# Seventh product of every second Strassen unit: weights 64 bytes further on in their tile

## The chip, the cores and the metric

The kernel runs on one core of one Trainium2 chip. The metric is the device time of one execution in microseconds. Three runs of the kernel before gave 2523.32, 2526.15 and 2526.63 us; the median is 2526.15 us. The profiled execution is a run of its own.

## The reference

Two layers of a macaron block over one sequence of 512 tokens with 1024 channels. Each layer is a half-weighted feed-forward block, a mixer of three branches (RWKV-7 time mixing, chunked gated linear attention, cross-attention into 256 memory rows) merged under sigmoid gates, and a second feed-forward block:

```python
for l in range(DEPTH):                                   # DEPTH = 2
    x = x + 0.5 * swiglu_ffn(rmsnorm(x, ffn1_norm[l]), ffn1_w_in[l], ffn1_w_out[l])
    h = rmsnorm(x, mix_norm[l])
    ...                                                  # three branches, gates
    x = x + merged @ w_out[l]
    x = x + 0.5 * swiglu_ffn(rmsnorm(x, ffn2_norm[l]), ffn2_w_in[l], ffn2_w_out[l])
return rmsnorm(x, final_norm)

def swiglu_ffn(h, w_in, w_out):                          # D_FF = 2816
    gate, up = jnp.split(h @ w_in, 2, axis=-1)
    return (jax.nn.silu(gate) * up) @ w_out
```

What matters here are the three large products of a layer: `h @ w_in` and `... @ w_out` of the four feed-forward blocks, and `merged @ w_out` at the mixer's end. All is float32.

## The kernel before

All activations lie transposed: channels on the 128 partitions, the 512 tokens along the free axis. A float32 product is made from three products of the rounded type `float32r`: an operand is split into `hi`, its rounded value, and `lo`, the rest (`Net.split`: ScalarE writes `hi`, VectorE writes `lo`), and hi·hi, hi·lo and lo·hi are summed in PSUM.

The large products run as Strassen units (in the form with seven products). `Net.seven` (line 906) describes one unit. It takes weights as four blocks of n·128 columns per partition (n is 4, or 3 in the last third of the feed-forward's second product) and makes seven products of 256 tokens each. Their sums grow in three PSUM tiles, X, Y and Z. The unit is cut in three functions: `begin` makes the first two products, `middle` the next three, and `end` the last two. `Net.chain` (line 957) calls them so that `begin` of the next unit stands ahead of `end` of the present one. There are 30 units in each of the four feed-forward blocks (the first four columns of its first product are made without Strassen) and 4 at the end of each mixer, 128 in all.

`self.par7` turns with each unit, and `par` is its value for the unit; it is true for the first, third, fifth unit and so on. Before the change `par` chooses one thing alone, the PSUM tile of Z.

One product is `Net.part`: for each of the n weight blocks of 128x128 two matmuls with the rounded weights (against the operand's `hi` and `lo`), and then for each block one with the weights' rest, so 12 matmuls with n = 4, and 9 with n = 3. Each has a load of its weights of its own. The weights are the stationary operand, the activations (256 columns) stream.

`Net.piece` (line 839) makes the `hi` and `lo` of a block of weights. A pair of blocks gets two tiles from a shared pool. A single block (the fifth, sixth and seventh product of a unit) gets one tile `hl` with 64 + 2·512 numbers per partition from a ring of two (`fhl`); `hi` stands at `SHIFT` = 48 numbers, 192 bytes, from its start, and `lo` 512 numbers behind `hi`. The seventh product's weights come raw by a DMA on SyncE's queue into a tile `d` and need no sum of blocks, so `hl<-d` in the profile is the split of the seventh product's weights and nothing else. Its matmuls are those of ps_i (the tile of Y) with `hl`, just ahead of the next unit's `middle`.

The order of all instructions comes from a list scheduler in the kernel. `Recorder` notes every operation with its dependences (from which parts of a tile it reads and writes, `overlap`), `Recorder.cost` gives each a duration from engine, operation and element count, and `Recorder.plan` simulates the queues six times and keeps the shortest order. Matmuls are taken in the order in which they were noted, where they are ready. Because all operations are issued by one loop, the profile shows one line, L317, for nearly all of them, and groups are told apart by tiles.

Two small tiles exist for place alone: `shift` (48 numbers) and `level` (16 numbers), allocated in `setup` ahead of other pools. Places along a partition are the sum of the sizes that stand before.

Of the kernel before, what the change touches and what calls it, by code (L numbers as in the profile page):

```python
# [20 lines left out]
T = 512  # L21
# [10 lines left out]
SHIFT = 48  # L32
# [562 lines left out]
class Net:  # L595
# [240 lines left out]
        ops["t3"] = [(t3[0][:, q], t3[1][:, q]) for q in range(4)]  # L836
        return ops

    def piece(self, pool, raw):

        if raw.shape[1] == 2:
            hi, lo = (self.wp.tile(list(raw.shape), F32R, name=t[1:], tag=t, bufs=2) for t in ("whi", "wlo"))
        else:
            n = raw.shape[2]
            f = pool.tile([P, 64 + 2 * T], F32R, name="hl", tag="fhl", bufs=2)
            hi, lo = (f[:, SHIFT + i * T:SHIFT + i * T + n].rearrange("p (c t) -> p c t", c=1) for i in range(2))
        self.split(hi, lo, raw)
        return [(hi[:, c, :], lo[:, c, :]) for c in range(raw.shape[1])]

# [56 lines left out]
    def seven(self, pool, src, n, ops, evict, clear=False):  # L906


        nc, C = self.nc, n * P
        self.par7 = not self.par7  # L910
        par = self.par7
        ring = lambda tag, bufs, k=2: pool.tile([P, k, C], F32, name=tag, tag=tag, bufs=bufs)

        def begin():
            w = src.rearrange("p (c t) -> p c t", c=4)
            a = self.wp.tile([P, 2, C], F32, name="wraw", tag="wraw", bufs=3)
            nc.sync.dma_start(out=a, in_=w[:, 0:2])
            nc.gpsimd.dma_start(out=a[:, 1], in_=w[:, 3], accum_op=ALU.add)
            q = ring("q", NQ)
            nc.sync.dma_start(out=q[:, 1], in_=w[:, 2])  # L920
            e = ring("q", NQ)
            nc.sync.dma_start(out=e[:, 0], in_=w[:, 1])
            nc.gpsimd.dma_start(out=e[:, 0], in_=w[:, 0], accum_op=ALU.add)
            d = ring("d", 2, 1)
            nc.sync.dma_start(out=d, in_=w[:, 3:4])
            X, Y = self.big()[:, :H], self.small("i")[:, :H]
            Z = self.small("fc"[par])[:, :H]
            v = self.piece(pool, a)
            self.part(X, v[0], ops["b11"], True)
            if clear:  # L930
                nc.tensor.matmul(Y, v[0][0][:, :P], ops["b11"][0][0], start=True, stop=True)
            nc.scalar.activation(Y, X, AF.Copy)
            nc.vector.tensor_tensor(q[:, 0], a[:, 1], a[:, 0], ALU.add)
            self.part(Z, v[1], ops["n1"], True)
            evict("z1", Z)
            return q, e, d, X, Y, Z

        def middle(q, e, d, X, Y, Z):
            v = self.piece(pool, q)
            self.part(Y, v[0], ops["n2"], False)  # L940
            evict("u2", Y)
            nc.vector.tensor_tensor(e[:, 1], q[:, 0], q[:, 1], ALU.add)
            self.part(X, v[1], ops["b21"], False)
            evict("x", X)
            self.part(Y, self.piece(pool, e[:, 0:1])[0], ops["t3"], False)
            evict("u3", Y)
            return d, e, Y, Z

        def end(d, e, Y, Z):
            self.part(Z, self.piece(pool, e[:, 1:2])[0], ops["b22"], False)  # L950
            evict("z", Z)
            self.part(Y, self.piece(pool, d)[0], ops["t4"], False)
            evict("y", Y)

        return begin, middle, end

    def chain(self, jobs):
# [959 lines left out]
```

## Time and profile before

| what | us |
|---|---|
| median of three runs | 2526.15 |
| profiled execution, all | 2527.82 |
| its span, first to last instruction | 2526.0 |
| TensorE matmul busy | 2502.3 |
| TensorE weight load busy | 2265.2 |
| VectorE busy | 2100.2 |
| ScalarE busy | 1471.5 |
| GpSimd busy | 241.4 |

A busy time is the union of the instructions' spans on an engine. Matmuls overlap in the array, so the length of one says little of the pace; the pace is read from start to start, or from the chain of work, where a stretch of matmuls of one tile is given with its start, its length and its number. The time line lists single instructions in the same form.

### The profile page before, as it was taken

To read this page: it belongs to the slowest core of one execution; us is meant where nothing else is said; L and a number is where in the kernel's file an instruction comes from. 1 tells how busy PE (TensorE), PEld (TensorE's weight loads), DVE (VectorE), ACT (ScalarE), POOL (GpSimd) and SP (SyncE) were. 2 spreads that over 40 slices of the span, in tenths; PEclk is the share of its full clock that TensorE was granted. 3 is DMA by queue.
4 is the path that set the end of the run, shared out by engine and by line. 5 is a ranking of instruction groups with operands and counts; after the bars stand their busy time and mean duration, and the time that the engine had idled before them with its cause. 6 is when DMAs were issued, how large, how long until landed. Compare 5 with 4: busy or idle time off the path is not lost.

```text
span 2526.0 us, 47194 instructions
## 1 busy us (share of the span) xinstructions
PE 2502.3 (99%) x17636; PEld 2265.2 (90%) x17636; DVE 2100.2 (83%) x4218; ACT 1471.5 (58%) x2660; POOL 241.4 (10%) x364
## 2 busy tenths in 40 slices
PE   9999999999999999999999999999999999999998
PEld 8999988888888799999989999877887888899998
DVE  8988886678888689888899888766888877898888
ACT  6665666564544456565665656674745434565655
POOL 1111100000000001211111111000000000012110
PEclk9999999999999999999999999999999999999999
DMA  7787762322222556877657777523222225468774
GB/s 199 201 197 187 166 189 82 117 73 70 78 77 73 144 157 154 206 189 182 149 144 197 189 184 173 175 88 97 83 69 88 67 78 172 134 164 207 188 180 103
DMA packets 163668, 358.02 MB, mean 142 GB/s; under 512 B 18256, under 2 KB 38160, under 8 KB 163440
## 3 DMA queue, kind: packets, MB, share of 16 engines
q1 hardware_dynamic: 125344, 288.87, 36.7%
q0 software_dynamic: 36864, 65.03, 16.0%
q8 instruction: 139, 2.28, 0.4%
q10 hardware_dynamic: 1232, 1.11, 0.1%
q14 instruction: 89, 0.73, 0.1%
HBM read 342.88 MB, written 12.06 MB: 141 GB/s over the span
## 4 chain that ended last, share of the span: by engine, by line
PE 88%; DVE 7%; DMA 2%; issue 1%; ACT 1%; SPq 0%; DVEq 0%; ACTq 0%; POOLq 0%
PE ps_b L317 42%; PE ps_i L317 26%; PE ps_f L317 10%; PE ps_c L317 9%; PE ps_y L317 1%; DVE wlo L317 1%; DVE x L317 1%; DVE ml L317 0%; DMA q<-in_ffn_out_dram 0%; ACT whi L317 0%; DMA q<-in_ffn_in_dram 0%; DVE hl L317 0%; DVE S L317 0%; DVE sqa L317 0%; DMA q<-in_w_out_dram 0%
## 5 line engine op out<-in xcount | busy, mean ns | idle before, releaser
L317 PE MATMUL ps_b<-xhi,whi 128*128 128x512 f32 (+1 forms) x880 | 354.4, 403 | 0.0
L317 PE MATMUL ps_b<-xlo,whi 128*128 128x512 f32 (+1 forms) x880 | 353.0, 401 | 0.1
L317 PE MATMUL ps_b<-xhi,wlo 128*128 128x512 f32 x864 | 347.7, 402 | 0.6 <-DVE wlo L317 0.6
L317 DVE TENSOR_TENSOR wlo<-wraw,whi 128x1024 fp32r<-128x1024 f32 (+1 forms) x172 | 183.6, 1068 | 75.9 <-ACT whi L317 71.6
L317 ACT ACTIVATE hl<-q 128x512 fp32r<-128x512 f32 (+1 forms) x256 | 158.0, 618 | 138.4 <-PE ps_i L317 40.3
L317 ACT ACTIVATE whi<-wraw 128x1024 fp32r<-128x1024 f32 (+1 forms) x174 | 161.7, 930 | 130.4 <-PE ps_b L317 100.1
L317 ACT ACTIVATE hi<-wraw 128x1024 fp32r<-128x1024 f32 (+2 forms) x162 | 166.3, 1026 | 100.8 <-PE ps_i L317 40.6
L317 DVE TENSOR_TENSOR lo<-wraw,hi 128x1024 fp32r<-128x1024 f32 (+2 forms) x162 | 191.3, 1181 | 37.9 <-ACT hi L317 36.9
L317 PEld LDWEIGHTS ps_b<-xlo,whi 128*128 128x128 f32 (+1 forms) x880 | 164.2, 187 | 35.9 <-DVE xlo L317 2.5
L317 PEld LDWEIGHTS ps_b<-xhi,whi 128*128 128x128 f32 (+1 forms) x880 | 164.6, 187 | 33.3 <-issue 1.2
L317 PEld LDWEIGHTS ps_b<-xhi,wlo 128*128 128x128 f32 x864 | 162.8, 188 | 33.3 <-DVE wlo L317 1.9
L317 DVE TENSOR_TENSOR hl<-q,hl 128x512 fp32r<-128x512 f32 (+1 forms) x256 | 170.4, 667 | 12.7 <-ACT hl L317 11.9
L317 ACT ACTIVATE hi<-q 128x1024 fp32r<-128x1024 f32 (+1 forms) x128 | 132.0, 1031 | 76.8 <-PE ps_b L317 56.9
L317 DVE TENSOR_TENSOR lo<-q,hi 128x1024 fp32r<-128x1024 f32 (+1 forms) x128 | 151.8, 1186 | 24.9 <-ACT hi L317 24.4
L317 PE MATMUL ps_i<-mh,hl 128*128 128x256 f32 x832 | 166.5, 281 | 1.7 <-ACT hl L317 1.0
L317 PE MATMUL ps_b<-xhi,hi 128*128 128x256 f32 x576 | 141.9, 279 | 0.0
L317 PE MATMUL ps_b<-xlo,hi 128*128 128x256 f32 x576 | 141.9, 279 | 0.0
L317 PEld LDWEIGHTS ps_i<-mh,hl 128*128 128x128 f32 x832 | 134.7, 188 | 3.0 <-ACT hl L317 1.5
L317 DVE TENSOR_TENSOR q<-q 128x512 f32<-128x512 f32 (+1 forms) x128 | 85.5, 668 | 41.1 <-DMA q<-in_ffn_in_dram 35.4
L317 ACT ACTIVATE hl<-d 128x512 fp32r<-128x512 f32 (+1 forms) x128 | 79.0, 617 | 59.6 <-PE ps_i L317 36.0
L317 PE MATMUL ps_i<-t,hl 128*128 128x256 f32 x864 | 113.3, 279 | 0.0
L317 PE MATMUL ps_i<-xhi,hl 128*128 128x256 f32 x576 | 113.3, 279 | 0.0
(424 smaller groups left out, 7223.6 us busy)
## 6 DMA issues: line engine op xcount, KB each, us to landing
wraw<-in_w_main_dram SPq DMA_DIRECT2D x108, 512.0 KB, 3.6
wraw<-in_ffn_in_dram SPq DMA_DIRECT2D x102, 512.0 KB, 4.6
q<-in_ffn_in_dram SPq DMA_DIRECT2D x144, 256.0 KB, 4.3
d<-in_ffn_in_dram SPq DMA_DIRECT2D x72, 256.0 KB, 3.9
q<-in_ffn_in_dram POOLq DMA_DIRECT2D x72, 256.0 KB, 6.0
wraw<-in_ffn_in_dram POOLq DMA_DIRECT2D x72, 256.0 KB, 4.9
wraw<-in_ffn_out_dram SPq DMA_DIRECT2D x32, 512.0 KB, 4.3
q<-in_ffn_out_dram SPq DMA_DIRECT2D x64, 256.0 KB, 3.5
```

What stands on the lines that cost most here:

```text
L317: return getattr(getattr(self.tc.nc, engine), what)(*(f(v) for v in a), **{n: f(v) for n, v in k.items()})
```

## The change

`piece` gets a parameter `at`, the place of `hi` in the tile, which is `SHIFT` unless given. `middle` hands `par` on to `end`, and `end` asks for the seventh product's weights at `SHIFT + 16` where `par` is true. 16 numbers of 4 bytes are 64 bytes. `lo` moves along, since it stands `T` numbers behind.

```diff
-    def piece(self, pool, raw):
+    def piece(self, pool, raw, at=SHIFT):
...
             f = pool.tile([P, 64 + 2 * T], F32R, name="hl", tag="fhl", bufs=2)
-            hi, lo = (f[:, SHIFT + i * T:SHIFT + i * T + n].rearrange("p (c t) -> p c t", c=1) for i in range(2))
+            hi, lo = (f[:, at + i * T:at + i * T + n].rearrange("p (c t) -> p c t", c=1) for i in range(2))
...
-            return d, e, Y, Z
-
-        def end(d, e, Y, Z):
+            return d, e, Y, Z, par
+
+        def end(d, e, Y, Z, par):
             self.part(Z, self.piece(pool, e[:, 1:2])[0], ops["b22"], False)
             evict("z", Z)
-            self.part(Y, self.piece(pool, d)[0], ops["t4"], False)
+            self.part(Y, self.piece(pool, d, SHIFT + 16 if par else SHIFT)[0], ops["t4"], False)
             evict("y", Y)
```

## The prediction

> **What bounds the kernel now.** The view of cores comes first: it says whether the clock was held back. Then the page's first part (busy shares) and its fourth (the chain of work that ended last).
>
> ```profile
> core 0: 2526.0 us, clock 0.998
> ```
>
> ```profile
> PE 2502.3 (99%) x17636; PEld 2265.2 (90%) x17636; DVE 2100.2 (83%) x4218; ACT 1471.5 (58%) x2660; POOL 241.4 (10%) x364
> ...
> PE 88%; DVE 7%; DMA 2%; issue 1%; ACT 1%; SPq 0%; DVEq 0%; ACTq 0%; POOLq 0%
> PE ps_b L317 42%; PE ps_i L317 26%; PE ps_f L317 10%; PE ps_c L317 9%; PE ps_y L317 1%; DVE wlo L317 1%; DVE x L317 1%; DVE ml L317 0%; DMA q<-in_ffn_out_dram 0%; ACT whi L317 0%; DMA q<-in_ffn_in_dram 0%; DVE hl L317 0%; DVE S L317 0%; DVE sqa L317 0%; DMA q<-in_w_out_dram 0%
> ```
>
> TensorE holds 88% of the chain, at a clock of 0.998, and each matmul has a weight load of its own (17636 of both). So the time is a number of matmuls times the distance from one start to the next. That distance, not the "mean ns of one" of the page (279 ns for 256 columns, which contains the pipeline's depth), is what the change can touch. The chain in order of time gives it: start, length, what, number. First a late stretch of Strassen units, then one in which PE runs otherwise:
>
> ```profile
> 2461.59 1.41 PE ps_c L317 x12
> 2463.01 1.41 PE ps_f L317 x12
> 2464.42 2.83 PE ps_i L317 x24
> 2467.24 1.41 PE ps_b L317 x12
> ```
>
> ```profile
> 1366.27 2.72 PE ps_i L317 x24
> 1368.99 1.36 PE ps_b L317 x12
> 1370.35 1.57 PE ps_i L317 x12
> 1371.92 1.41 PE ps_b L317 x12
> ```
>
> A matmul of 256 columns follows the one before after 2.83/24 = 117.9 ns as a rule, and after 2.72/24 = 113.3 ns in a few short stretches. The same products, from the same tiles, run at both paces. The quick pace ends at 1370.35, where a group starts with a delay (1.57 against 1.41, 0.16 us), and the usual pace follows. So PE has **two steady paces**, 4.6 ns apart, and an event at the seam of two products can move it from one to the other. The usual one holds nearly everywhere, and after most delays PE falls back into it.
>
> **The change part by part.** It moves `hl`, the rounded weights and their rest of the seventh product, by 16 numbers (64 bytes) in every unit with `par` true. The tile has 64 + 2·512 = 1088 numbers; the two pieces now stand at 64 to 575 and 576 to 1087, still inside and still apart. The tile keeps its size, so no other tile moves. The list scheduler reads engines, element counts and overlaps, not places, so the order on all queues, the waits and all DMAs stay as they are: nothing is added, removed or re-ordered. What remains is the cost of the same instructions at another place.
>
> How many they are, from the view of the instructions that touch `d`:
>
> ```profile
> L317 ACT ACTIVATE hl<-d x128: 508/633/636, 60.4 to 2510.6; 128x512 fp32r<-128x512 f32 x112, 128x384 fp32r<-128x384 f32 x16
> L317 DVE TENSOR_TENSOR hl<-d,hl x128: 543/681/695, 64.0 to 2511.2; 128x512 fp32r<-128x512 f32 x112, 128x384 fp32r<-128x384 f32 x16
> ```
>
> 128 units, 112 with four weight blocks (12 matmuls in the seventh product) and 16 with three (9 matmuls). `par` turns with each unit, so half of both kinds is moved: 56·12 + 8·9 = **744 matmuls** with as many weight loads, 64 writes of ACT and 64 of DVE.
>
> *The writes.* ACT and DVE write the moved pieces. Their nearest rows are writes of the same form to other tiles, `xhi` and `xlo`, which stand 64 bytes otherwise in the memory than `hl` does:
>
> ```profile
> L317 DVE TENSOR_TENSOR xlo<-xt,xhi 128x512 fp32r<-128x512 f32 x32 | 21.8, 681 | 0.0
> ...
> L317 ACT ACTIVATE xhi<-xt 128x512 fp32r<-128x512 f32 x32 | 19.2, 624 | 7.8 <-DVE xt L317 7.8
> ```
>
> 681 ns against a median of 681, and a mean of 624 against a median of 633: no difference that could be told. And they are covered, as the time line around one seventh product shows (start, length):
>
> ```profile
> 2461.37 0.68 DVE L317 TENSOR_TENSOR hl<-d,hl 128x512 fp32r<-128x512 f32 x1
> ...
> 2464.14 0.19 PEld L317 LDWEIGHTS ps_i<-xhi,hl 128*128 128x128 f32 x1
> 2464.26 0.28 PE L317 MATMUL ps_i<-xhi,hl 128*128 128x256 f32 x1
> ...
> 2465.67 0.51 PE L317 MATMUL ps_i<-n,hi 128*128 128x256 f32 x3
> ```
>
> DVE is done at 2462.05 and the first load reads at 2464.14: 2.1 us of cover, three times the write itself. I take 0 for the writes; without that cover, 64 writes slower by a tenth (0.07 us) would cost 4.5 us.
>
> *The weight loads and matmuls.* The twelve run from 2464.26 to 2465.67, 1.41 us, 117.5 ns each: the usual pace. In the layout of this kernel all weights of the Strassen units stand 128 bytes past a multiple of 256 and all operands that stream against them 192 past one; by the change 744 loads stand at 192 too, the same place as what streams. The trace has a few matmuls with this relation already: those of `wl` and `al` against `wzh` and `wzl` in the mixer, also 256 columns wide. Two of their sixteen groups:
>
> ```profile
> 527.53 0.39 PE L317 MATMUL ps_b<-xhi,whi 128*128 128x512 f32 x1
> 527.76 0.28 PE L317 MATMUL ps_i<-wl,wzh 128*128 128x256 f32 x1
> 527.88 0.28 PE L317 MATMUL ps_i<-wl,wzl 128*128 128x256 f32 x1
> 528.00 0.28 PE L317 MATMUL ps_i<-al,wzh 128*128 128x256 f32 x1
> 528.12 0.28 PE L317 MATMUL ps_i<-al,wzl 128*128 128x256 f32 x1
> 528.24 0.40 PE L317 MATMUL ps_b<-xlo,whi 128*128 128x512 f32 x1
> ```
>
> ```profile
> 1811.64 0.28 PE L317 MATMUL ps_i<-wl,wzh 128*128 128x256 f32 x1
> ...
> 1812.11 0.38 PE L317 MATMUL ps_f<-pt,vm 128*128 128x256 f32 x1
> ```
>
> Four matmuls in 0.48 us (120 ns each), four in 0.47 us (118 ns). They come in fours, between other shapes, so this is no steady run; but it is the nearest row. The bounds per moved matmul: from below, the quick pace, 113.3 - 117.9 = -4.6 ns (-3.4 us over 744), if the new place lets them run at it; from above, the slower of the two rows and as much again for what fours can't show, about +4 ns (+3.0 us). I take the slower row, +2 ns, because all four of its distances are a full 120: 744 · 2 = **1.5 us**.
>
> Here two rules of the Trainium skill speak. "SBUF — State Buffer", section Specifications, gives lines of 16 bytes as what an engine's reads cross; a shift of 64 bytes is four whole lines, and by that rule the sum would be 0. "TensorE: Matmul & The Clock Gate", section "Step-by-step: what each phase is for", says that the weight load and the moving operand have a read port each, so that a load takes nothing from the matmul beside it; by that too it would be 0. The Trainium skill gives there no reason for two paces with the same tiles, which the rows of the chain show.
>
> *The seams.* At 64 places PE goes over to moved weights and at 64 back to unmoved ones. A seam that throws no state costs nothing that could be seen: the pace before and after it is the same. I take 0; both ends are in the rivals.
>
> The sum is +1.5 us on a span of 2526.0. The profiled execution took 2527.82 in all, 1.82 around the span, and would take 2529.3. Against the median of the runs, 2526.15 (1.67 under the profiled one), that is 2527.65, so **2527.7 us**, +0.06%. A measurement of this kernel can tell about 0.2%, 5.05 us, from no change.
>
> **The rivals.**
>
> *Nothing at all* (0 us, 2526.2). Loads run at the same pace from the new place, and the seams throw nothing. For it: the writes' equal durations, and the 118 ns of the second group. Against it: the 120 ns of the first.
>
> *The quick pace is thrown on* (faster). The new place, or the seam back from it, sets the phase between loads and matmuls so that PE goes on at 113.3 ns. All 64 seams are alike, so either most do this or few. For it: the chain shows that the quick pace exists, and that it lasts over whole products once begun (24 + 12 at 1366.27). Against it: PE falls back into the usual pace after nearly every delay, and a seam of places is no delay. Price: if the unit after each moved product ran quickly, 64 · 84 matmuls (seven products of 12) · 4.6 ns = 24.7 us, so 2501; if it held until the next moved product, 156 matmuls, it would be 45.9 us, 2480. From 1098 quick matmuls on (5.05 us / 4.6 ns), 17 a seam, it is more than a measurement's bound.
>
> *The seam breaks the overlap* (slower). The going over from one place to the other delays a load once, and PE's queue starts anew as at 1370.35, where a delayed group took 0.16 us more. At one of the two seams of a unit that is 64 · 0.16 = 10.2 us, so 2536; at both, 2547. It decides from 0.08 us a unit. For it: the loads' busy share of 90% leaves little room, and the distance between starts hangs on the load as well as on the matmul. Against it: the seam from `whi` to `wzh` at 527.53 to 528.24 shows no such step, and neither does the one from ps_f to ps_i in the late stretch. That the change doesn't do what it says is ruled out by the sizes above.
>
> **How the numbers follow.** The chances: the forecast 0.44, nothing at all 0.08, the quick pace 0.30, the broken overlap 0.18. The first two are both within 0.2% (0.52); the third is faster (0.30), the fourth slower (0.18). The likeliest case's own range goes from -3.4 to +3.0 us around 2526.15, with the spread of the runs (2523.3 to 2526.6) on top: 2521 to 2531. To leave out no more than 2 in 10, the range reaches up to the fourth rival's 2536 and half of its spread, 2538, and down to 2502, which takes in the weak forms of the quick pace (up to 81 quick matmuls a seam), and leaves out the strong ones and a broken overlap at both seams.
>
> **What the next profile would show.** Right: the counts of the page unchanged; the chain's groups of 24 on ps_i, of which 12 are a seventh product, at 2.83 in every second unit and about 2.85 in the others; all others as before. The quick pace: rows of 1.36 x12 and 2.72 x24 behind moved products over long stretches. The broken overlap: a longer group, 1.5 or more x12, once a unit pair. The prediction is wrong if the pace of groups that are not moved changes, and its step on the writes is wrong if PE waits for `hl` there.

## The result and the profile after

The median of five runs is 2515.82 us (2510.16 to 2516.33). The ratio to the kernel before is 0.9952, 95% interval 0.9937 to 0.9967: 10.3 us faster. The forecast was 2527.7, no change. The profiled execution of after took 2510.16, the quickest of its five, 17.7 under the profiled execution of before, so its trace shows more of the effect than the median has.

The view of cores, and the first and fourth part of the page:

```profile
core 0: 2508.1 us, clock 0.999
```

```profile
PE 2486.0 (99%) x17636; PEld 2247.4 (90%) x17636; DVE 2098.3 (84%) x4218; ACT 1468.7 (59%) x2660; POOL 241.3 (10%) x364
...
PE 53%; DVE 3%; issue 1%; ACT 0%; DMA 0%; DVEq 0%; ACTq 0%; SPq 0%
```

Every count is that of before, and so is the clock. TensorE's busy time fell by 16.3 us (2502.3 to 2486.0), nearly the whole of the span's 17.9, while VectorE's and ScalarE's fell by 2 and 3. (The chain was followed back through only a part of the span this time; its shares are not to be set beside those of before.) So the same matmuls ran closer together. Where, the chain in order of time shows (start, length, what, number):

```profile
2239.62 1.41 PE ps_f L317 x12
2241.04 1.41 PE ps_c L317 x12
2242.45 2.79 PE ps_i L317 x24
2245.24 1.36 PE ps_b L317 x12
2246.60 1.36 PE ps_i L317 x12
2247.96 1.36 PE ps_b L317 x12
```

Two products at the usual pace (1.41), then on ps_i twelve moved matmuls and the next unit's first twelve. 2.79 is neither 2.83 (all usual) nor the foretold 2.85: the twelve moved ones take 1.43 and the twelve behind them 1.36. From there on the quick pace of 113.3 ns holds, in products that the change doesn't touch. The time line of PE around another moved product shows the single steps:

```profile
164.54 0.28 PE L317 MATMUL ps_i<-xhi,hl 128*128 128x256 f32 x1
164.65 0.28 PE L317 MATMUL ps_i<-xlo,hl 128*128 128x256 f32 x1
164.77 0.28 PE L317 MATMUL ps_i<-xhi,hl 128*128 128x256 f32 x1
...
165.97 1.07 PE L317 MATMUL ps_i<-n,hi 128*128 128x256 f32 x8
...
167.33 0.28 PE L317 MATMUL ps_b<-xhi,hi 128*128 128x256 f32 x1
```

Moved: 164.54 to 165.97, 1.43 us for 12, 119.2 ns each. Behind it, unmoved: 165.97 to 167.33, 1.36 us for 12, 113.3 ns each. Among the 256-column matmuls of the large products the moved ones are now the slowest, and those behind them the quickest.

To count this over the whole kernel, all distances from start to start of neighbouring `float32r` matmuls of 256 columns were taken from each trace (10,665 of the 17,636 matmuls) and sorted: quick up to 115 ns, usual 116 to 125, and above that a delay, of which the part over the pace is summed.

| kernel | quick | usual | delays (sum over the pace, us) | all such distances, us |
|---|---|---|---|---|
| before | 391 | 10,199 | 75 (9.5) | 1264.0 |
| after | 5,438 | 5,082 | 145 (15.9) | 1249.4 |

5047 more quick ones at 117.8 - 113.35 = 4.45 ns make -22.5 us. The 744 moved ones, at a mean of 119.1 ns, make +1.0. Delays give back +6.4. That is -15.1, and the distances fell by 14.6, most of the span's 17.9. The 64 moved products stand in 72 unbroken stretches, since a few are interleaved with others; in what follows a stretch is counted as entered, and left, at the pace of the few distances just before and just behind it. (The counts move by one to three with the number of distances taken.)

The further delays are met at the quick pace: 62 delays (6.9 us) follow the quick pace, where 13 (1.5 us) did before; those that follow the usual pace are 54 and were 45 (6.1 and 6.4 us). The view of waits of the weight loads names one new wait among them (total us, times, longest):

```profile
PEld ps_i L317 <- ACT ft L317: 2.0, 5, 1.0
```

Before, the same view has no such row. That is a part of the 6.4 us; which waits the rest are was not followed. How a stage looks, one row of the windows view of each kernel shows, before and after (window, its length, busy time and number of instructions of PE, PEld, DVE, ACT and POOL, granted clock, DMA share, GB/s):

```profile
1300.00:1580.00 280.00, 279.91 (x2354) 278.45 (x2354) 249.58 (x462) 174.84 (x319) 48.34 (x56) 1.00 0.76 186
```

```profile
1300.00:1580.00 280.00, 279.39 (x2405) 278.02 (x2404) 251.71 (x470) 175.74 (x323) 46.61 (x54) 1.00 0.77 189
```

In the same 280 us PE starts 2405 matmuls instead of 2354, 2.2% more, at the same granted clock and busy time. Busy shares can't show this.

### The profile page after: what moved, and what is told of

Read it like the earlier page. It is cut to its first block, busy times and chain, and to the rows that moved or that the text cites. A ratio compares the mean times of both kernels' runs of the same rounds, so it can differ in the third digit from the quotient of the medians.

```text
span 2508.1 us, 47188 instructions
## 1 busy us (share of the span) xinstructions
PE 2486.0 (99%) x17636; PEld 2247.4 (90%) x17636; DVE 2098.3 (84%) x4218; ACT 1468.7 (59%) x2660; POOL 241.3 (10%) x364
## 4 chain that ended last, share of the span: by engine, by line
PE 53%; DVE 3%; issue 1%; ACT 0%; DMA 0%; DVEq 0%; ACTq 0%; SPq 0%
PE ps_b L317 24%; PE ps_i L317 17%; PE ps_f L317 6%; PE ps_c L317 5%; PE ps_y L317 1%; DVE wlo L317 0%; DVE x L317 0%; DMA mt<-in_mem_dram 0%; DMA q<-in_ffn_in_dram 0%; DVE S L317 0%; DVE hl L317 0%; ACT whi L317 0%; DVE t L317 0%; DVE xlo L317 0%; DVE xn L317 0%
```

## The experiments

Eleven kernels were run. Each edit is against the changed kernel; the work and its order are the same in all, only places differ. "Place" below means bytes past a multiple of 256: before, all Strassen weights stand at 128 and all streamed operands at 192. Ratios are to the kernel before, run on the same chip.

| label | weights moved | median us | ratio (95%) | quick | delays (us) |
|---|---|---|---|---|---|
| e1_all_moved | all, +64 bytes, no seams | 2543.45 | 1.0067 (1.0055–1.0079) | 14 | 35 (4.6) |
| e2_rest_only | rests of the 7th, +64, every 2nd unit | 2526.58 | 0.9993 (0.9984–1.0002) | 256 | 74 (9.1) |
| e3_every_unit | 7th, +64, every unit | 2509.59 | 0.9932 (0.9920–0.9944) | 6,208 | 136 (14.0) |
| e4_back64 | 7th, -64, every 2nd | 2524.67 | 0.9991 (0.9982–0.9999) | 643 | 73 (9.5) |
| e5_rounded_every | rounded part of the 7th, +64, every unit | 2514.23 | 0.9946 (0.9934–0.9959) | 5,852 | 164 (21.3) |
| e6_two_products | 6th and 7th, +64, every 2nd | 2516.13 | 0.9955 (0.9942–0.9968) | 5,526 | 129 (15.7) |
| e7_every_fourth | 7th, +64, every 4th | 2519.81 | 0.9964 (0.9952–0.9977) | 3,108 | 130 (18.2) |
| e8_scan | 7th, at 17 places in turn | 2524.34, one run | – | 1,861 | 111 (12.3) |
| e9_back128 | 7th, -128, every 2nd | 2512.60 | 0.9946 (0.9934–0.9959) | 6,246 | 158 (21.0) |
| e10_singles128 | 5th to 7th, -128, every unit | 2505.53 | 0.9922 (0.9908–0.9935) | 8,866 | 179 (24.4) |
| e11_all128 | all, by 128, no seams | 2522.28 | 0.9985 (0.9975–0.9994) | 5,710 | 163 (23.5) |

### Place or seam?

**e1_all_moved.** All Strassen weights, and the mixer's pairs, 64 bytes on. There is no going over between places left. The pad behind `rt` keeps all other tiles at their places past 256.

```diff
-        nc.gpsimd.memset(self.shift.tile([P, SHIFT], F32, name="shift", tag="shift"), 0.0)
+        nc.gpsimd.memset(self.shift.tile([P, SHIFT + 16], F32, name="shift", tag="shift")[:, :SHIFT], 0.0)
...
-        rt = self.nrm.tile([P, nt], F32, name="rt", tag="rt", bufs=2)
+        rt = self.nrm.tile([P, 28], F32, name="rt", tag="rt", bufs=2)[:, :nt]
...
-    def piece(self, pool, raw, at=SHIFT):
+    def piece(self, pool, raw, at=SHIFT + 16):
...
-            self.part(Y, self.piece(pool, d, SHIFT + 16 if par else SHIFT)[0], ops["t4"], False)
+            self.part(Y, self.piece(pool, d, SHIFT + 16)[0], ops["t4"], False)
...
-                            self.root = self.nrm.tile([P, 4], F32, name="rt", tag="rt", bufs=2)
+                            self.root = self.nrm.tile([P, 28], F32, name="rt", tag="rt", bufs=2)[:, :4]
```

> Every weight tile of the Strassen units, and of the mixer, stands 64 bytes further on, and what streams stays: no unit has a seam between two places any more. Seam theory (the quick pace of 113.3 ns is thrown on where PE goes back from moved to unmoved weights, and the moved place itself costs 2 ns): no quick stretches beyond the few of before, about 119.9 ns for matmuls of 256 columns throughout, so 10,600 x 2 = 21 us and something for the 512-column ones: 2545 to 2565 us. Place theory (matmuls run quicker because their weights stand there): as fast as the changed kernel or faster, 2516 us or less. Lottery theory (any other layout draws the stretches of quick pace anew): between 2505 and 2530 us.

Measured: 2543.45, slower by 0.67%. Its chain in order of time has one pace:

```profile
2240.00 1.44 PE ps_c L317 x12
2241.44 1.44 PE ps_i L317 x12
2242.88 1.44 PE ps_b L317 x12
...
2250.08 2.88 PE ps_i L317 x24
```

1.44/12 and 2.88/24 are 120.0 ns, throughout (10,616 distances, mean 120.0, 14 quick ones). The sum of all distances grew by 20.1 us (1264.0 to 1284.1), near the 21 foretold; the whole stayed just under the seam theory's range, since the 512-column matmuls became no slower (229.0 ns against 229.8). So the new place is not a better place: by itself it is the **slowest** of the three paces. The gain of the change comes from going over between places.

**e3_every_unit.** Twice as many seams.

```diff
-            self.part(Y, self.piece(pool, d, SHIFT + 16 if par else SHIFT)[0], ops["t4"], False)
+            self.part(Y, self.piece(pool, d, SHIFT + 16)[0], ops["t4"], False)
```

> The seventh product's weights are moved in every unit, 1488 matmuls and 128 seams back instead of 64. Seam theory: after a delay that ended it the quick pace comes back one unit earlier, so some 6500 of 9100 unmoved matmuls are quick against 5400 of 9800, less 1.5 us for the moved ones: 2507 to 2514 us. Place theory: twice the gain, 2505 us. Lottery theory: between 2505 and 2530 us.

Measured: 2509.59 (2507.20 to 2513.94), as the seam theory asked, with 6208 quick matmuls although 1488 are now moved ones at the slow pace.

**e7_every_fourth.** Half as many, 32.

```diff
+        self.unit = getattr(self, "unit", -1) + 1
+        moved = self.unit % 4 == 0
...
-            self.part(Y, self.piece(pool, d, SHIFT + 16 if par else SHIFT)[0], ops["t4"], False)
+            self.part(Y, self.piece(pool, d, SHIFT + 16 if moved else SHIFT)[0], ops["t4"], False)
```

> The seventh product is moved in every fourth unit, 32 seams. If the quick pace lasts until a delay or the next seam, as the stretches in the changed kernel look, about half of its gain: 2518 to 2523 us. If it lasted only for the product behind the seam, a quarter of it or less: above 2523 us. If nothing but a delay ended it and delays were rare: 2513 to 2517 us.

Measured: 2519.81. With 0, 32, 64 and 128 moved products the quick matmuls are 391, 3108, 5438 and 6208: 85 more a moved product with 32, 79 with 64, and only 12 for each of the second 64. In e3_every_unit PE enters 77 stretches quickly already, which have nothing left to win.

### How many matmuls does it take?

**e2_rest_only.** Only the weights' rests of the seventh product are moved, the last 4 (or 3) of its matmuls, in every second unit.

```diff
-            hi, lo = (f[:, at + i * T:at + i * T + n].rearrange("p (c t) -> p c t", c=1) for i in range(2))
+            hi, lo = (f[:, a + i * T:a + i * T + n].rearrange("p (c t) -> p c t", c=1) for i, a in ((0, SHIFT), (1, at)))
```

> In every second unit only the rest of the seventh product's weights is moved (4 or 3 matmuls at its end, 248 in all, instead of 744); the rounded weights stay. Seam theory: the seam back to unmoved weights is the same, so the quick share is as in the changed kernel and the 2 ns are paid by a third of the matmuls, 2513 to 2517 us against 2516. Place theory: a third of the gain, about 2522 us. Lottery theory: anywhere between 2505 and 2530 us.

Measured: 2526.58, no change. The chain behind the seams stays usual:

```profile
2235.72 2.83 PE ps_i L317 x24
2238.54 1.41 PE ps_b L317 x12
...
2245.61 2.83 PE ps_i L317 x24
```

Of 63 stretches that PE entered at the usual pace, none was left quickly. The plain seam theory, "any going over throws it", fell here. What stands after it: PE has to run some matmuls at the moved place before it leaves that quickly.

**e5_rounded_every.** The opposite part: the rounded weights (8 of 12 matmuls) in every unit. `hi` and `lo` change their halves of the tile in all single products, which leaves the places past 256.

```diff
-            hi, lo = (f[:, at + i * T:at + i * T + n].rearrange("p (c t) -> p c t", c=1) for i in range(2))
+            lo, hi = (f[:, a + i * T:a + i * T + n].rearrange("p (c t) -> p c t", c=1) for i, a in ((0, SHIFT), (1, at)))
...
-            self.part(Y, self.piece(pool, d, SHIFT + 16 if par else SHIFT)[0], ops["t4"], False)
+            self.part(Y, self.piece(pool, d, SHIFT + 16)[0], ops["t4"], False)
```

> In every unit only the rounded weights of the seventh product are moved (its first 8 or 6 matmuls, 992 in all), the rest stays. Lock theory (at the moved place PE settles into an even pace of 120.0 ns of its own, at once when it comes from the quick pace and after about seven matmuls from the usual one; only from there does going back throw the quick pace on): eight are just enough, so the quick share is that of the run with every unit, a third fewer matmuls pay, 2504 to 2512 us. If the whole product is needed, or the seam has to stand at a product's end: 2522 to 2528 us.

Measured: 2514.23, just above the 2504 to 2512 of the expectation. The throw is there: of 66 stretches entered at the usual pace 39 are left quickly, as against 37 of 55 in e3_every_unit; eight matmuls do. Against e3_every_unit it lacks 4.6 us, and its delays are 7.3 us more (21.3 against 14.0).

**e6_two_products.** The sixth and the seventh moved, 24 in a row.

```diff
-            self.part(Z, self.piece(pool, e[:, 1:2])[0], ops["b22"], False)
+            self.part(Z, self.piece(pool, e[:, 1:2], SHIFT + 16 if par else SHIFT)[0], ops["b22"], False)
```

> In every second unit the sixth and the seventh product are moved, 24 matmuls in a row instead of 12, 64 seams back as in the changed kernel. Lock theory: what has not settled to 120.0 ns after 12 matmuls does so in 24, so nearly all 64 seams throw the quick pace on (43 of 64 in the changed kernel), over 60% of the unmoved matmuls are quick (55% there), and 744 more moved matmuls pay: 2510 to 2516 us. Entry theory (the phase at which the moved product is entered decides, however long it is): again two in three seams, 2517 to 2523 us.

Measured: 2516.13, at the border between the two ranges, so the count decides: 25 of 46 stretches entered at the usual pace are left quickly, against 27 of 45 in the changed kernel. A longer stay throws no oftener. Single distances in the trace of the changed kernel show what goes with it: entered from the usual pace, the moved matmuls either settle (117, 118, 119, 121, 117, 117, then 120 five times, and 114, 113, 113 behind the seam) or run in a cycle of five (121, 120, 124, 117, 118) that doesn't end before the product does. From the quick pace they settle at once (114, 119, then 120 ten times), and 25 of 25 went on quickly. Of the 56 moved products there that ran without a break, 47 had settled by their end and all 47 were left quickly; nine were still in the cycle and all nine were left at the usual pace. So it is **how PE enters**, and not how long it stays, that goes with the outcome.

### Which places?

**e4_back64** and **e9_back128.** The other way, by 64 and by 128 bytes.

```diff
-            self.part(Y, self.piece(pool, d, SHIFT + 16 if par else SHIFT)[0], ops["t4"], False)
+            self.part(Y, self.piece(pool, d, SHIFT - 16 if par else SHIFT)[0], ops["t4"], False)
```

> The change with the other sign: 64 bytes back instead of on, in every second unit. Seam theory, if any difference of place throws the quick pace on: 2510 to 2518 us. If it depends on the direction (the load of the first unmoved matmul must come later against what streams): no quick stretches behind the seams, 2525 to 2531 us. Place theory: at this place too the moved matmuls would have to be quick, 113 ns in the moved products.

```diff
-            self.part(Y, self.piece(pool, d, SHIFT + 16 if par else SHIFT)[0], ops["t4"], False)
+            self.part(Y, self.piece(pool, d, SHIFT - 32 if par else SHIFT)[0], ops["t4"], False)
```

> The change with 128 bytes back instead of 64 on. In the scan, all seven moved products at this place ran at 113.3 ns, after three or four matmuls where they came from the usual pace, and all went on at 113.3 behind it. If that is so for all 64 units: nothing paid for the moved matmuls and every seam throws: 2503 to 2511 us against 2516. If the seven were chance, as often as in the changed kernel (two in three): 2511 to 2516 us.

Measured: e4_back64 2524.67, where none of 64 stretches is left quickly; e9_back128 2512.60, where 34 of 40 entered at the usual pace are. By its time e9_back128 lies in the range for a throw in two of three; by the count it throws oftener, though not at every seam, and its delays grew too (21.0 us). A seam alone does nothing; it must lead to certain places.

**e8_scan.** The seventh product of successive units at 17 places from 192 bytes back to 64 on, in steps of 16; it ran once.

```diff
+        self.unit = getattr(self, "unit", -1) + 1
+        place = 4 * (self.unit * 5 % 17)
...
-            self.part(Y, self.piece(pool, d, SHIFT + 16 if par else SHIFT)[0], ops["t4"], False)
+            self.part(Y, self.piece(pool, d, place)[0], ops["t4"], False)
```

> The seventh product's weights stand at another place in each unit, 0 to 64 numbers from the tile's start in steps of four (16 bytes), 17 places in turn, six to eight units each. One look, for the pace inside the moved product and behind it by place. Lock theory: places with an even pace inside, all steps alike, are those behind which the quick pace can follow; 64 bytes on is one of them. If any change of place throws it on, stretches of 113 ns follow many places; 64 bytes back had none.

Measured, as units left quickly of units at that shift (counted from the trace; -192 and +64 are the same place):

| shift, bytes | left quickly |
|---|---|
| -128 | 7 of 7 |
| -96 | 5 of 8 |
| +64 or -192 | 13 of 15 |
| -16 | 2 of 7 |
| +16 | 1 of 8 |
| 0 | 0 of 7 |
| the other ten | 0 of 76 |

Three places throw, and the shifts of 16 bytes beside each of them (-144, -112, -80, +48, and -176, which is +80 past 256) don't. The lottery theory, by which any other layout draws the quick stretches anew, falls with this: the outcome goes with the place, 7 of 7 at one and 0 of 76 at ten. At -128 PE is quick within the moved product already, as the time line of one shows:

```profile
1463.44 0.28 PE L317 MATMUL ps_i<-xhi,hl 128*128 128x256 f32 x1
1463.56 0.28 PE L317 MATMUL ps_i<-xlo,hl 128*128 128x256 f32 x1
1463.68 0.28 PE L317 MATMUL ps_i<-xhi,hl 128*128 128x256 f32 x1
1463.80 0.28 PE L317 MATMUL ps_i<-xlo,hl 128*128 128x256 f32 x1
1463.91 0.28 PE L317 MATMUL ps_i<-xhi,hl 128*128 128x256 f32 x1
1464.02 0.28 PE L317 MATMUL ps_i<-xlo,hl 128*128 128x256 f32 x1
...
1464.82 0.28 PE L317 MATMUL ps_i<-mh,hi 128*128 128x256 f32 x1
```

Three distances of 120 ns, and then 110 (the view rounds to 10). All twelve take 1.38 us (1463.44 to 1464.82), 115 ns each. So at this place a moved product costs nothing; it gains.

**e10_singles128.** Hence the fifth, sixth and seventh product of every unit at this place. The pairs of blocks stay, and with them the seams.

```diff
-    def piece(self, pool, raw, at=SHIFT):
+    def piece(self, pool, raw, at=SHIFT - 32):
...
-            self.part(Y, self.piece(pool, d, SHIFT + 16 if par else SHIFT)[0], ops["t4"], False)
+            self.part(Y, self.piece(pool, d, SHIFT - 32)[0], ops["t4"], False)
```

> The fifth, sixth and seventh product of all units stand 128 bytes back, 4464 matmuls, in two stretches a unit. If the place has 113.3 ns as its only steady pace and the usual place keeps it until a delay: over 85% of the 10,600 matmuls quick, 45 us by count, less what other engines then let PE wait for (the wait time grew by 7 us where 5000 were quick): 2492 to 2503 us. If only the seam counts and not the place: as the run with every unit, 2507 to 2514 us.

Measured: 2505.53 (2505.05 to 2506.81), ratio 0.9922, the **best** of all: 19.8 us under the median of before on the same chip (2525.29). The ratio of the change is 0.9952. The time lies between the two ranges foretold. 8866 distances (83%) are quick. By their number this is worth 8475 · 4.45 = 37.7 us, and 14.9 of it come back as delays. The chain in order of time, with its shares over the window, shows whose:

```profile
by line: PE ps_i L317 38.8%; PE ps_b L317 25.9%; PE ps_f L317 14.9%; PE ps_c L317 13.3%; DVE s L317 1.8%; DVE lo L317 1.6%; DVE ml L317 1.1%; DVE hl L317 1.0%; ACT mh L317 0.8%; DVE fm L317 0.4%; ACT ft L317 0.4%; issue 0.1%; DVEq L317 0.0%
...
2228.90 2.72 PE ps_i L317 x24
2231.62 1.36 PE ps_b L317 x12
2232.98 1.59 PE ps_i L317 x12
...
2242.80 1.68 PE ps_i L317 x12
2244.48 1.41 PE ps_b L317 x12
```

The same view of the changed kernel, over the same window, is PE alone:

```profile
by line: PE ps_i L317 42.3%; PE ps_b L317 30.2%; PE ps_f L317 14.2%; PE ps_c L317 13.6%
```

At the quick pace PE overtakes the splits and sums of VectorE and ScalarE (1.59 and 1.68 instead of 1.36), and behind the delay at 2242.80 it is back at the usual pace (1.41): a delay costs its own length, and can cost the pace. Of 120 delays met at the quick pace in this kernel, 65 left PE at the usual one and 55 did not. In e9_back128 the weights' transfers are in the chain too, over the same stretch:

```profile
2256.63 1.13 DVE lo L317
2266.46 1.14 DVE lo L317
2269.82 5.61 DMA wraw<-in_ffn_in_dram
2275.99 8.15 DMA wraw<-in_ffn_in_dram
```

**e11_all128.** All weights at that place, no seams.

```diff
-        nc.gpsimd.memset(self.shift.tile([P, SHIFT], F32, name="shift", tag="shift"), 0.0)
+        nc.gpsimd.memset(self.shift.tile([P, SHIFT + 32], F32, name="shift", tag="shift")[:, :SHIFT], 0.0)
...
-        rt = self.nrm.tile([P, nt], F32, name="rt", tag="rt", bufs=2)
+        rt = self.nrm.tile([P, 20], F32, name="rt", tag="rt", bufs=2)[:, :nt]
...
-    def piece(self, pool, raw, at=SHIFT):
+    def piece(self, pool, raw, at=SHIFT - 32):
...
-            self.part(Y, self.piece(pool, d, SHIFT + 16 if par else SHIFT)[0], ops["t4"], False)
+            self.part(Y, self.piece(pool, d, SHIFT - 32)[0], ops["t4"], False)
...
-                            self.root = self.nrm.tile([P, 4], F32, name="rt", tag="rt", bufs=2)
+                            self.root = self.nrm.tile([P, 20], F32, name="rt", tag="rt", bufs=2)[:, :4]
```

> All weights of the Strassen units and of the mixer stand 128 bytes further on (the same place modulo 256 as 128 back), no seams. If the place decides: as quick as the run before this one or a little quicker in the units, but the 512-column matmuls of the mixer come to a relation at which the few that have it took 233 ns against 229.7, 3500 times 3 ns = 11 us: 2500 to 2512 us. If seams are needed: usual pace, 2525 us or more.

Measured: 2522.28, ratio 0.9985. Both paces live at this place, and a delay ends the quick one here as well:

```profile
2233.08 2.72 PE ps_i L317 x24
2237.16 1.56 PE ps_i L317 x12
2238.72 1.41 PE ps_b L317 x12
...
2242.96 2.83 PE ps_i L317 x24
```

5710 distances are quick and 4792 usual. So this place alone, with no seam, gives as many quick matmuls as the change does (5438). A delay not only ends the quick pace here but also begins it: of the 25 times that PE came back to it for five distances or more, 19 came right behind one or more delays. Of the delays met at the usual pace 23 of 41 left PE at the quick one, and 1 of 45 in the kernel before. The time lies between the ranges of the two theories, and neither holds as it stood: seams aren't needed at this place, and the place alone doesn't hold the quick pace either. A second cost shows: the 512-column matmuls, whose weights were moved too, went from a mean of 229.8 ns to 233.1, about +11 us in sum. That e10_singles128 did better (8866 quick) can come from its seams or from the weights that it left in place; a kernel with the Strassen weights alone at this place was not run.

## Why the prediction was wrong

**What held.** The counts and the order of work didn't change, and the writes of ACT and DVE cost nothing that shows: their busy times fell. The price of a moved matmul held: foretold +2 ns from the mixer's four distances of 120, measured 119.1 against 117.8 (+1.3) in the change and 120.0 (+2.2) in the steady run of e1_all_moved. 1.5 us were foretold for the 744, 1.0 were measured. There was luck in the choice of the row: over all sixteen groups of the mixer the distances have a mean of 118.1 (40 of them, delays left out). The reading that PE has two steady paces, 117.9 and 113.3, held in each kernel but e1_all_moved, which has a third. One sum was off without bearing on the rest: by its own terms the likeliest case's range is 2519.9 to 2529.6, not 2521 to 2531.

**The step that failed** is the one on the seams: "A seam that throws no state costs nothing that could be seen: the pace before and after it is the same. I take 0." The pace behind the seam is *not* that of before it. Of 45 stretches of moved matmuls that PE entered at the usual pace 27 were left at the quick one, and of 25 entered quickly all. That term is 5047 matmuls · 4.45 ns = -22.5 us in the profiled execution.

**The rival that held** is that the quick pace is thrown on. Its count was near: 64 · 84 = 5376 matmuls foretold for one unit behind each seam, 5047 measured, 79 a seam where 17 were enough. That nearness is in part luck: 18 of the 45 stretches entered at the usual pace weren't left quickly, and the quick pace often lasted past one unit, up to the next moved product. Its time, 2501, was too low, because it left out what the quick pace brings with it: delays grew by 6.4 us, and of the 62 met at the quick pace 55 ended it. And the profiled run was the quickest of five; the median shows 10.3 us.

**The argument against it** was the fault: "PE falls back into the usual pace after nearly every delay, and a seam of places is no delay." The first half held where the weights stand at 128 (9 of 13 before, 55 of 62 after), though not at the place 128 bytes back (65 of 120 in e10_singles128). The second half took it that only a delay can move PE between its paces. The trace of before shows otherwise. Of the five times that PE went over from the usual to the quick pace there (for five distances or more), four have neither a delay nor weights at another place ahead of them, at 1014.89, 1247.65, 1349.36 and 2268.44 us. Around the first of them the chain reads

```profile
1012.23 2.12 PE ps_i L317 x18
1014.35 2.18 PE ps_b L317 x19
```

which is 117.8 ns a matmul and then 114.7, without a gap. What moved PE there is open. In the change a moved product that enters from the usual pace can settle at a third pace, 120, and each unbroken one that did so was left quickly. That the even run at another pace brings PE into a new phase is a reading of this, and not shown; at -128 bytes there is no third pace, and PE is quick within the product. I had the third pace in hand: the mixer's 120 ns was read as a price of 2 ns and not as another rhythm that PE must leave again.

**The broken overlap** was wrong. With 64 moved products there is no delay at each seam: single distances over a settled seam read 120, 121, 113. Of the 70 further delays, 49 are met at the quick pace (62 against 13).

**The rules weighed.** By "SBUF — State Buffer" of the Trainium skill, section Specifications, a shift by four whole 16-byte lines was taken to cost 0. The runs disagree: with shifts by whole lines, e1_all_moved goes at 120.0 ns and e11_all128 at 113.3 and 117.8. "TensorE: Matmul & The Clock Gate" of the Trainium skill, section "Step-by-step: what each phase is for", with a read port each for weights and streamed operand, gave 0 as well; in these runs the pace does hang on where the weights stand (113.3, 117.8 or 120.0 ns). The streamed operands stood at 192 throughout, so whether it is the place itself or the distance between the two was not tested, and no run here shows where inside the chip it comes from.

**What stays open.** Why these places throw, among them the one at -96, where the moved product itself runs unevenly (115 to 120 ns); what the paces are in the hardware; and why runs of one program differ (2510.16 to 2516.33 for the change, 2510.16 to 2523.39 for e7_every_fourth): each kernel has one trace, so that a different number of throws in each run explains it is argued only.

## What to carry to other kernels

Read TensorE's pace from start to start and look whether the same products run at two paces; if they do, a busy share of 99% still hides some per cent, and what moves PE from one pace to the other was worth more here (-22.5 us) than the price of the moved instructions (+1.0). A change of address alone, with no instruction changed, was worth 0.8% here (e10_singles128) and cost 0.7% (e1_all_moved), so weights are worth trying at several places past 256 bytes, and in a mixture as well as all at one. When the bounding engine gets quicker, count what it then waits for: 6.4 of 22.5 us came back as delays here, 14.9 of 37.7 in the best version.

## What the hardware showed that was not expected

- A stream of 256-column `float32r` matmuls, each with a weight load of its own, has at least three steady paces at the same granted clock (0.998 to 0.999): 113.3, 117.8 and 120.0 ns. The third is the only one when weights and streamed operand stand at the same place past 256 bytes (14 quick distances of 10,665 in e1_all_moved).
- With weights at another place, at 128 or 0, both other paces exist, and the pace in which PE is mostly goes on until something disturbs it. How a delay leaves it goes with the place: with the weights at 128 nearly always at the usual pace (4 of 58 delays left it quick in the kernel before), at 0 more often at the quick one (83 of 138 in e11_all128). Some matmuls at another place can also leave it at the quick pace. Of the stretches at +64 entered at the usual pace, twelve and 24 matmuls did so about equally often (27 of 45, 25 of 46), eight did (39 of 66), the last four never (0 of 63).
- The throw is sharp in the address: 7 of 7 at -128 bytes, 5 of 8 at -96, and 0 of 15 at -112 and -80.
- 512-column matmuls feel the place too, by less: means of 229.8 ns before, 229.0 with all weights 64 bytes on, 233.1 with all of them 128 on.
